# Every second piece of an up-projection's weights gets its low part from an adding DMA

## Chip, cores and metric

The kernel runs on one core of one Trainium2 chip. The metric is the device time of one execution in microseconds (us); the time before is the median of three runs, 1161.08 us (1160.6 to 1163.76). A core has a matrix engine (TensorE: PE in the profile, its weight loads PEld), VectorE (DVE), ScalarE (ACT), GpSimd (POOL), SyncE (SP), which here only issues DMAs, and 16 DMA engines. Each engine works through its own instructions in a fixed order; semaphores order the engines among each other.

## The reference, cut to what matters

One layer of a hybrid encoder, for 256 tokens of width 2048, everything in float32:

```
h  = rms_norm(x);  p = h @ w_in                      # 2048 x 6152
x  = x + concat(norm(fox_attention), norm(stick_breaking)) @ w_out
h  = rms_norm(x);  u = h @ w_up                      # 2048 x 11264
u  = causal_depthwise_conv(u, width 3) + conv_b
gate, val = split(u, 2)
x  = x + (silu(gate) * val) @ w_down                 # 5632 x 2048
```

The change sits in `u = h @ w_up`.

## The kernel before, in words

**Two parts.** TensorE is fed in a reduced 32-bit format (float32r). To keep the accuracy, each operand is split in two: a high part, the value rounded to that format, and a low part, the value minus the high part. A product is the sum of high times high, high times low and low times high.

**Pieces of weights.** All weights come through `weights` (L202): 204 pieces, mostly of 128 partitions x 2048 elements (1 MB). SP issues the load into `w_raw` (L209; three buffers), ScalarE rounds it into `w_hi` (L210; two buffers), VectorE writes `w_lo` = `w_raw` - `w_hi` (L211; two buffers), and TensorE multiplies. So a `w_raw` buffer is free for the load three pieces on once VectorE's L211 has read it, and a `w_hi` buffer is free once TensorE is through with the piece two before. The three instructions are given a priority that lets the scheduler place them ahead of other work (AHEAD = 200); the order on each engine is otherwise the scheduler's, fixed when the kernel is built.

**The up-projection.** `feature_major` (L244) computes two tiles of 128 features for the 256 tokens from two pieces (`kh` 0 and 1, each 8 row blocks of 128 x 256 columns, so rows of 1 KB in memory). A piece is 16 times a matmul with `w_hi` over both parts of the activations (512 columns, L258) and a matmul with `w_lo` over the high part (256 columns, L262), in this order: the first low matmul is the second matmul of a piece. The last argument `spare` is true in the up-projection alone, where there are 88 pieces. After two pieces, `convolved` (L580) takes the sums out of PSUM (ACT L586, DVE L587 and L588) and applies the convolution (ACT L590, DVE L594); after four, the gate is applied and split into `g2` (L615 to L619; 24 buffers).

**The order of the feed-forward.** Three parts of 16, 16 and 12 feature tiles (FFN_PARTS): up-projection of a part (32, 32 and 24 pieces), then its down-projection (`token_major`, L220; 16, 16 and 12 pieces). Before them stand the projections and attention, then the output projection, whose last column block is followed by squares of the rows (ACT L167) and by transposes that fill `hT` (PE L152, ACT L157, DVE L158) for the up-projection. The pool `ff` (L573) takes over the memory that the attention's pools had.

Of the kernel before, what the change touches and what calls it, by code (L numbers as in the profile page):

```python
# [9 lines left out]
F32R = mybir.dt.float32r  # L10
AF = mybir.ActivationFunctionType
ALU = mybir.AluOpType
# [16 lines left out]

# Columns of the constant array.  # L30
C_ID, C_TRI, C_ONE = (P * i for i in range(3))
# [12 lines left out]
def hybrid_layer(  # L44
# [34 lines left out]
    def f32(t):  # L79
        return t.bitcast(F32)  # L80

# [1 line left out]
    NC2 = 2 * NFT  # L83
# [48 lines left out]

# [1 line left out]
    pcol = const.tile([P, 50], F32, name="pcol")  # L134
# [12 lines left out]
    def transposed_split(k, g):  # L147
        """Feature tiles k and k + 1 of the tokens' rows, transposed, times g, in two parts."""
        ps = psb.tile([P, 2, S], F32, name="ps_x", tag="t")
        for j in range(2):  # L150
            for t in range(NT):
                nc.tensor.transpose(  # L152
                    ps[:, j, t * P : (t + 1) * P], xt[t][:, (k + j) * P : (k + j + 1) * P], ident
                )
        for j in range(2):
            i = k + j
            act.activation(hT[:, i, 0, :], ps[:, j, :], AF.Identity, scale=g[:, i : i + 1])  # L157
            dve.scalar_tensor_tensor(  # L158
                hT[:, i, 1, :], ps[:, j, :], g[:, i : i + 1], f32(hT[:, i, 0, :]),
                op0=ALU.mult, op1=ALU.subtract,  # L160
            )

    def sums_of_squares(ss, c):
        """Of 512 columns of each token tile."""
        for t in range(NT):
            junk = tmp.tile([P, 512], F32, name="junk", tag="raw", bufs=4)
            act.activation(junk, xt[t][:, c * 512 : (c + 1) * 512], AF.Square, accum_out=ss[:, t, c : c + 1])  # L167

    def token_factors(ss, n):
        """1 / rms of each token: per partition, and in every partition."""  # L170
        rstd = const.tile([P, NT], F32, name=f"rstd{n}")
        ssum = small.tile([P, NT], F32, name="ssum", tag="ssum")
        dve.tensor_reduce(ssum, ss, axis=AX.X, op=ALU.add)
        rsqrt(rstd, ssum, 1.0 / D, NT)
        dg = []
        for t in range(NT):
            dg.append(small.tile([P, P], F32, name="dg", tag="dg", bufs=2))
            dve.tensor_scalar(dg[t], ident, rstd[:, t : t + 1], None, op0=ALU.mult)
        return rstd, dg
# [8 lines left out]

# [1 line left out]
    waiting = deque()  # L190
# [9 lines left out]

# [1 line left out]
    def weights(src, a, b):  # L202
        raw = wpool.tile([P, 2048], F32, name="w_raw", tag="w_raw")
        hi = wpool.tile([P, 2048], F32R, name="w_hi", tag="w_hi", bufs=2)
        lo = wpool.tile([P, 2048], F32R, name="w_lo", tag="w_lo", bufs=2)
        n = a * b
        r3 = raw[:, :n].rearrange("p (a b) -> p a b", a=a)
        with tc.high_priority(offset=AHEAD):
            nc.sync.dma_start(r3, src)  # L209
            act.copy(hi[:, :n], raw[:, :n])  # L210
            dve.tensor_tensor(lo[:, :n], raw[:, :n], f32(hi[:, :n]), op=ALU.subtract)  # L211
        return (
            hi[:, :n].rearrange("p (a b) -> p a b", a=a),
            lo[:, :n].rearrange("p (a b) -> p a b", a=a),
        )
# [4 lines left out]
    def token_major(lhs, w, k0, nk, c0, cols, pieces=None, before=None):  # L220
        """[tokens, cols] = lhs.T @ w[k0:k0+nk, c0:c0+cols] for both token tiles."""
        acc = [psa.tile([P, 512], F32, name=f"acc{t}", tag="acc") for t in range(NT)]
        k = 0
        for n in pieces or [4] * (nk // 4):
            if before:
                before(k, n)
            hi, lo = weights(rows_of(w, k0 + k, n, c0, cols), n, cols)
            for i in range(n):
                first, last = k + i == 0, k + i == nk - 1
                lh = lhs(k + i)  # L230
                for t in range(NT):
                    lhi = lh[:, 0, t * P : (t + 1) * P]
                    llo = lh[:, 1, t * P : (t + 1) * P]
                    o = acc[t][:, :cols]
                    nc.tensor.matmul(o, lhi, hi[:, i, :], start=first, stop=False)  # L235
                    nc.tensor.matmul(o, lhi, lo[:, i, :], start=False, stop=False)  # L236
                    nc.tensor.matmul(o, llo, hi[:, i, :], start=False, stop=last)  # L237
            k += n
            step()
        return acc  # L240
# [3 lines left out]
    def feature_major(w, c0, spare):  # L244
        """Two tiles of features, each [features, tokens] in two summands."""
        nonlocal n_acc
        acc = []
        for j in range(2):
            pool, tag = (psa, "acc") if n_acc % 3 or not spare else (psb, "s")
            acc.append(pool.tile([P, 512], F32, name="pu", tag=tag))  # L250
        n_acc += 1
        for kh in range(2):
            hi, lo = weights(rows_of(w, 8 * kh, 8, c0, 2 * P), 8, 2 * P)
            for i in range(8):
                k = 8 * kh + i
                for j in range(2):
                    fs = slice(j * P, (j + 1) * P)
                    nc.tensor.matmul(  # L258
                        acc[j], hi[:, i, fs], hT[:, k].rearrange("p a b -> p (a b)"),
                        start=k == 0, stop=False,  # L260
                    )
                    nc.tensor.matmul(  # L262
                        acc[j][:, S:], lo[:, i, fs], hT[:, k, 0, :], start=False, stop=k == KT - 1
                    )
            step()
        return acc

    with ExitStack() as actx:
# [9 lines left out]
        def to_heads(dst, rows, t, scale):  # L278
            """Four heads' [tokens, dims] to [dims, tokens], times scale."""
            ps = psb.tile([P, 4, P], F32, name="ps_h", tag="t")  # L280
# [4 lines left out]
        def fox_rows(acc, dst, g):  # L285
            """Queries or keys of four heads: normalised, then transposed."""
            rows = []
# [19 lines left out]

        # The last four heads come when the projections are through with hT, and are used up
        # before its last rows are written again.
        oT = [at.tile([P, 2, S], F32R, name=f"oT{h}") for h in range(2 * NH - 4)]  # L310
# [3 lines left out]
        def attended(po, h, g, group):  # L314
            """Output of a head, [dims, tokens]: times its norm's weight in two parts, and its squares."""
            o = oT[group * NH + h]
# [10 lines left out]

# [1 line left out]
        # The first columns of weights are taken as x arrives.  # L329
        def opening(k, n):  # L330
# [52 lines left out]
        def gates():  # L383
            # log_sigmoid(y) = min(y, 0) - ln(1 + exp(-|y|))
            la = tmp.tile([P, NT, NH], F32, name="la", tag="la")
# [7 lines left out]
            yield  # L393
            # Cumulative log gates, the head h of row r*8+h, over the tokens.
            pc = psb.tile([P, 512], F32, name="pc", tag="t")
# [71 lines left out]

# [1 line left out]
        B0 = 3 * WF + NH  # L469
# [15 lines left out]
        def sb_head(h, qT, kT, v):  # L485
# [8 lines left out]
            mm(z1, identR, maskS, start=False, stop=True)  # L494
            # softplus(z) = max(z, 0) + ln(1 + exp(-|z|))
            e = tmp.tile([P, 3 * P], F32, name="e", tag="pr")
# [8 lines left out]
            yield  # L505
            # z - sum of softplus over the keys from s on: the exponent of the weights.
            for i in range(2):
# [22 lines left out]

# [1 line left out]
        ss2 = const.tile([P, NT, 4], F32, name="ss2")  # L532
# [38 lines left out]

# [1 line left out]
    ff = ctx.enter_context(tc.tile_pool(name="ff", bufs=2))  # L573
# [6 lines left out]
    def convolved(ps, f):  # L580
        """Feature tile f after the up-projection, its token factor and its convolution."""
        nonlocal n_up
# [16 lines left out]
    def up_pair(f0):  # L599
        """Two feature tiles."""  # L600
        nonlocal R
# [7 lines left out]
    for n_part, (f_lo, f_hi) in enumerate(FFN_PARTS):  # L609
        for f in range(f_lo, f_hi, 2):  # L610
            gate = up_pair(f)
            val = up_pair(NFT + f)
            for j in range(2):
                sg = ff.tile([P, S], F32, name="sg", tag="sg")
                act.activation(sg, gate[j], AF.Silu)  # L615
                dve.tensor_tensor(sg, sg, val[j], op=ALU.mult)
                g2 = ff.tile([P, 2, S], F32R, name="g2", tag="g2", bufs=24)
                act.copy(g2[:, 0, :], sg)
# [66 lines left out]
```

## Time and profile before

| | |
|---|---|
| median of three runs | 1161.08 us |
| span of the profiled execution, first to last instruction (the profile has no other time of it) | 1158.9 us |
| granted TensorE clock, mean | 1.000 |
| bytes moved by DMA | 211.40 MB, 182 GB/s over the span |
| DVE busy, ACT busy, POOL busy | 732.1, 559.1, 0.2 us |

How to read it: busy time is the union of an engine's instructions. A row of the timeline gives the start in us from the span's start, the duration in us, engine, line, operation, output <- inputs, shapes and, in brackets, the idle time of the engine before it with what ended it. Matmul rows overlap each other, since matmuls are pipelined: what a matmul costs is the distance of two starts, not its own duration. "us to landing" of a DMA runs from its issue to its completion.

### The profile page before, as it was taken

What the parts mean: (1) busy time and instruction counts of PE and PEld (TensorE: products, weight loads), DVE (VectorE), ACT (ScalarE), POOL (GpSimd) and SP (SyncE); (2) the same over time, 40 slices, a digit from 0 to 9 for tenths busy, and PEclk for the clock granted to TensorE, in tenths of its full rate; (3) what the DMA queues carried; (4) which work ended last, traced back from release to release, by engine and by line L of the source; (5) the groups of instructions that cost most, each with busy time, mean ns of one, the idle gap of its engine ahead of it and who ended that gap; (6) DMA issues with size and microseconds to landing.
All of it is one profiled execution on the core that took longest, in us unless ns stands there. A gap on an engine that the chain in (4) does not pass through costs nothing.

```text
span 1158.9 us, 14648 instructions
## 1 busy us (share of the span) xinstructions
PE 1147.0 (99%) x6002; PEld 980.7 (85%) x6002; DVE 732.1 (63%) x960; ACT 559.1 (48%) x716; POOL 0.2 (0%) x4
## 2 busy tenths in 40 slices
PE   7999999999999999999999999999999999999998
PEld 5998888888888888888888888888888888888886
DVE  4646656556465667777774547777775456777753
ACT  4644444445564555555553335555554334555531
POOL 0000000000000000000000000000000000000000
PEclk9999999999999999999999999999999999999999
DMA  6666545554444555555556555655556655555662
GB/s 226 212 219 204 179 149 181 158 171 150 159 158 151 182 170 194 182 182 183 183 189 199 191 182 183 196 194 190 182 185 198 197 183 182 183 188 184 192 231 76
DMA packets 162540, 211.40 MB, mean 182 GB/s; under 512 B 3736, under 2 KB 117546, under 8 KB 162474
## 3 DMA queue, kind: packets, MB, share of 16 engines
q1 hardware_dynamic: 162474, 210.47, 56.5%
q8 instruction: 47, 0.77, 0.3%
q14 instruction: 19, 0.16, 0.0%
HBM read 208.36 MB, written 2.10 MB: 182 GB/s over the span
## 4 chain that ended last, share of the span: by engine, by line
PE 97%; DVE 1%; ACT 1%; DMA 0%; issue 0%; SPq 0%
PE pu L258 33%; PE pu L262 17%; PE acc L235 14%; PE acc L237 14%; PE acc L236 14%; DVE w_lo L211 1%; ACT w_hi L210 1%; PE ps_x L152 1%; DMA x<-in_x_dram 0%; PE ps_h L282 0%; PE ps_z L491 0%; PE ps_s L423 0%; PE ps_o L517 0%; PE ps_o L450 0%; PE ps_p L444 0%
## 5 line engine op out<-in xcount | busy, mean ns | idle before, releaser
L211 DVE TENSOR_TENSOR w_lo<-w_raw,w_hi 128x2048 fp32r<-128x2048 f32 (+2 forms) x204 | 450.7, 2210 | 341.1 <-ACT w_hi L210 340.8
L258 PE MATMUL pu<-hT,w_hi 128*128 128x512 f32 x1664 | 586.0, 397 | 0.0
L210 ACT CAST w_hi<-w_raw 128x2048 fp32r<-128x2048 f32 (+2 forms) x204 | 375.7, 1842 | 368.1 <-PE acc L237 164.7
L262 PE MATMUL pu<-hT,w_lo 128*128 128x256 f32 x1664 | 466.6, 281 | 0.1
L258 PEld LDWEIGHTS pu<-hT,w_hi 128*128 128x128 f32 x1664 | 312.1, 188 | 73.7
L262 PEld LDWEIGHTS pu<-hT,w_lo 128*128 128x128 f32 x1664 | 314.3, 189 | 0.7 <-DVE w_lo L211 0.5
L237 PE MATMUL acc<-w_hi,g 128*128 128x512 f32 x352 | 139.0, 395 | 0.0
L235 PE MATMUL acc<-w_hi,g 128*128 128x512 f32 x352 | 138.9, 395 | 0.0
L236 PE MATMUL acc<-w_lo,g 128*128 128x512 f32 x352 | 138.9, 395 | 0.0
L235 PE MATMUL acc<-w_hi,hT 128*128 128x512 f32 (+1 forms) x320 | 119.8, 376 | 0.0
L236 PE MATMUL acc<-w_lo,hT 128*128 128x512 f32 (+1 forms) x320 | 119.1, 372 | 0.1
L237 PE MATMUL acc<-w_hi,hT 128*128 128x512 f32 (+1 forms) x320 | 118.9, 372 | 0.0
L594 DVE SCALAR_TENSOR_TENSOR cv<-up,ccol,cv 128x256 f32<-128x256 f32 x176 | 84.3, 479 | 1.6 <-ACT cv L590 0.7
L237 PEld LDWEIGHTS acc<-w_hi,g 128*128 128x128 f32 x352 | 66.3, 188 | 15.7 <-DVE g L619 0.2
L235 PEld LDWEIGHTS acc<-w_hi,g 128*128 128x128 f32 x352 | 66.3, 188 | 15.5
L236 PEld LDWEIGHTS acc<-w_lo,g 128*128 128x128 f32 x352 | 66.3, 188 | 15.4
L236 PEld LDWEIGHTS acc<-w_lo,hT 128*128 128x128 f32 x320 | 60.5, 189 | 9.0 <-DVE w_lo L211 0.9
L237 PEld LDWEIGHTS acc<-w_hi,hT 128*128 128x128 f32 x320 | 60.6, 189 | 8.7
L235 PEld LDWEIGHTS acc<-w_hi,hT 128*128 128x128 f32 x320 | 60.5, 190 | 8.2
L586 ACT COPY t<-pu 128x256 f32<-128x256 f32 x88 | 31.5, 360 | 58.8 <-PE pu L262 58.8
L590 ACT ACTIVATE cv<-up,ccol 128x256 f32<-128x256 f32 x88 | 52.6, 597 | 7.9 <-DVE up L588 5.6
L587 DVE TENSOR_TENSOR t<-pu,t 128x256 f32<-128x256 f32 x88 | 36.8, 420 | 21.9 <-ACT t L586 21.9
(148 smaller groups left out, 648.3 us busy)
## 6 DMA issues: line engine op xcount, KB each, us to landing
w_raw<-in_w_up_dram SPq DMA_DIRECT2D x88, 1024.0 KB, 5.1
w_raw<-in_w_down_dram SPq DMA_DIRECT2D x44, 1024.0 KB, 5.3
w_raw<-in_w_in_dram SPq DMA_DIRECT2D x36, 1024.0 KB, 5.2
w_raw<-in_w_out_dram SPq DMA_DIRECT2D x16, 1024.0 KB, 5.1
w_raw<-in_w_in_dram SPq DMA_DIRECT2D x12, 688.0 KB, 5.1
w_raw<-in_w_in_dram SPq DMA_DIRECT2D x8, 512.0 KB, 5.2
out_dram<-x SPq DMA_DIRECT2D x8, 256.0 KB, 5.3
x<-in_x_dram SPq DMA_DIRECT2D x3, 512.0 KB, 6.1
```

The source lines that it names most:

```text
L152: nc.tensor.transpose(ps[:, j, t * P : (t + 1) * P], xt[t][:, (k + j) * P : (k + j + 1) * P], ident)
L210: act.copy(hi[:, :n], raw[:, :n])
L211: dve.tensor_tensor(lo[:, :n], raw[:, :n], f32(hi[:, :n]), op=ALU.subtract)
L235: nc.tensor.matmul(o, lhi, hi[:, i, :], start=first, stop=False)
L236: nc.tensor.matmul(o, lhi, lo[:, i, :], start=False, stop=False)
L237: nc.tensor.matmul(o, llo, hi[:, i, :], start=False, stop=last)
L258: nc.tensor.matmul(acc[j], hi[:, i, fs], hT[:, k].rearrange("p a b -> p (a b)"), start=k == 0, stop=False,)
L262: nc.tensor.matmul(acc[j][:, S:], lo[:, i, fs], hT[:, k, 0, :], start=False, stop=k == KT - 1)
L586: act.copy(t2, ps[:, S:])
L587: dve.tensor_tensor(t2, ps[:, :S], t2, op=ALU.add)
L590: act.activation(a, u[:, 2:], AF.Identity, scale=ccol[:, 2, f : f + 1], bias=ccol[:, 3, f : f + 1])
L594: dve.scalar_tensor_tensor(a, u[:, w : w + S], ccol[:, w, f : f + 1], a, op0=ALU.mult, op1=ALU.add)
```

## The change

In the up-projection, every second piece (the first of each two, 44 in all) gets its low part in another way: ScalarE writes minus the high part into a new tile `w_ld` (three buffers in the pool `ff`), then a DMA that GpSimd issues reads the same weights from memory once more and adds them to what stands in `w_ld`. The high part is made as before. VectorE has no instruction for these pieces. `g2` has 22 buffers in place of 24. The diff, without its removed comments:

```diff
-    def weights(src, a, b):
+    n_pieces = 0
+
+    def weights(src, a, b, shared=False):
+        nonlocal n_pieces
+        n_pieces += shared
         raw = wpool.tile([P, 2048], F32, name="w_raw", tag="w_raw")
         hi = wpool.tile([P, 2048], F32R, name="w_hi", tag="w_hi", bufs=2)
-        lo = wpool.tile([P, 2048], F32R, name="w_lo", tag="w_lo", bufs=2)
+        by_dma = shared and n_pieces % 2
+        if by_dma:
+            lo = ff.tile([P, 2048], F32R, name="w_ld", tag="w_ld", bufs=3)
+        else:
+            lo = wpool.tile([P, 2048], F32R, name="w_lo", tag="w_lo", bufs=2)
         n = a * b
         r3 = raw[:, :n].rearrange("p (a b) -> p a b", a=a)
         with tc.high_priority(offset=AHEAD):
             nc.sync.dma_start(r3, src)
-            act.copy(hi[:, :n], raw[:, :n])
-            dve.tensor_tensor(lo[:, :n], raw[:, :n], f32(hi[:, :n]), op=ALU.subtract)
+            if by_dma:
+                act.activation(lo[:, :n], raw[:, :n], AF.Copy, scale=-1.0)
+                nc.gpsimd.dma_start(
+                    lo[:, :n].rearrange("p (a b) -> p a b", a=a), src, accum_op=ALU.add
+                )
+                act.copy(hi[:, :n], raw[:, :n])
+            else:
+                act.copy(hi[:, :n], raw[:, :n])
+                dve.tensor_tensor(lo[:, :n], raw[:, :n], f32(hi[:, :n]), op=ALU.subtract)
...
-            hi, lo = weights(rows_of(w, 8 * kh, 8, c0, 2 * P), 8, 2 * P)
+            hi, lo = weights(rows_of(w, 8 * kh, 8, c0, 2 * P), 8, 2 * P, spare)
...
-                g2 = ff.tile([P, 2, S], F32R, name="g2", tag="g2", bufs=24)
+                g2 = ff.tile([P, 2, S], F32R, name="g2", tag="g2", bufs=22)
```

## Prediction

> **What bounds the kernel now.** I read the page first (busy times, the chain that ended last, the costliest groups, the DMA queues), then a table by stage, then the timeline of one stretch of the up-projection.
>
> ```profile
> span 1158.9 us, 14648 instructions
> PE 1147.0 (99%) x6002; PEld 980.7 (85%) x6002; DVE 732.1 (63%) x960; ACT 559.1 (48%) x716; POOL 0.2 (0%) x4
> ...
> q1 hardware_dynamic: 162474, 210.47, 56.5%
> ...
> PE 97%; DVE 1%; ACT 1%; DMA 0%; issue 0%; SPq 0%
> ...
> L211 DVE TENSOR_TENSOR w_lo<-w_raw,w_hi 128x2048 fp32r<-128x2048 f32 (+2 forms) x204 | 450.7, 2210 | 341.1 <-ACT w_hi L210 340.8
> ...
> L262 PEld LDWEIGHTS pu<-hT,w_lo 128*128 128x128 f32 x1664 | 314.3, 189 | 0.7 <-DVE w_lo L211 0.5
> ```
>
> TensorE is 97% of the chain, and its low weights waited for VectorE (last row, the wait named at its end) for 0.5 us in the whole kernel. By stage:
>
> ```profile
> core 0: us, PE busy (x) PEld busy (x) DVE busy (x) ACT busy (x) POOL busy (x), PEclk, DMA share, GB/s
> 430.00:590.00 160.00, 160.00 (x907) 138.68 (x906) 120.13 (x173) 85.39 (x114) 0.00 (x0) 1.00 0.57 184
> 700.00:850.00 150.00, 150.00 (x867) 132.25 (x866) 112.92 (x161) 80.14 (x107) 0.00 (x0) 1.00 0.58 190
> ```
>
> These are two stretches of the up-projection. TensorE has no gap in either, VectorE is 75% busy (120.13 of 160) and the DMA engines 57%. So the VectorE time that the change takes away stands beside TensorE's and is worth nothing; what counts is whether weights still arrive in time. One stretch of ACT, DVE and SP, put together from their timelines, then the landing times, and the DMA rate in 40 slices of 0.6 us from 500 to 524:
>
> ```profile
> 499.88 1.91 ACT L210 CAST w_hi<-w_raw 128x2048 fp32r<-128x2048 f32 x1 [2.67 <-issue]
> 501.82 2.29 DVE L211 TENSOR_TENSOR w_lo<-w_raw,w_hi 128x2048 fp32r<-128x2048 f32 x1 [1.55 <-ACT w_hi L210]
> 504.14 0.37 SPq L209 DMA_DIRECT2D w_raw<-in_w_up_dram  x1
> 516.84 1.91 ACT L210 CAST w_hi<-w_raw 128x2048 fp32r<-128x2048 f32 x1
> ```
> ```profile
> DMA to landing us min/median/max: 5.1/5.2/5.2
> ```
> ```profile
> GB/s 266 386 387 384 253 32 0 0 29 159 375 384 384 352 65 0 0 0 72 230 386 386 387 289 12 0 0 32 193 384 391 387 324 36 0 0 10 111 355 384
> ```
>
> From 499.88 to 516.84 are three pieces: 5.65 us a piece, 11.3 us a pair. VectorE ends at 504.11, the load for the piece three on is issued at 504.14 and lands 5.2 us later at 509.3; its cast starts at 516.84. So the loads are **7.5 us ahead**. A load runs at some 386 GB/s while it moves, 2.7 us for 1.05 MB, and 2.5 us of the 5.2 are latency.
>
> **The change, part by part.**
>
> *VectorE* loses 44 subtractions of 2.29 us, 101 us: worth 0, since TensorE hides them. At most the 0.5 us of its wait above.
>
> *ScalarE* gains 44 copies of 1.91 us (as the cast), 84 us. In the stretch 430 to 590 it is busy 85.39 of 160 us, 6.0 us a pair; 7.9 of 11.3 then fits. But order counts. In the built kernel the minus copy of a DMA piece (call it 2m+1) stands on ScalarE *ahead* of the cast of the piece before it (2m). It waits for the load of 2m+1, so the cast of 2m, VectorE's subtraction and TensorE now wait for a load that they don't use. This closes a ring: the `w_raw` buffer for 2m+1 comes free with VectorE's subtraction of 2m-2; then follow issue 0.03, landing 5.2, minus copy 1.91, cast of 2m 1.91, subtraction of 2m 2.29, and the next turn begins. Sum: 0.03 + 5.2 + 1.91 + 1.91 + 2.29 = **11.34 us per pair, against 11.3** that TensorE needs. A dead heat, as long as no load gets slower: each us on that load is a us on every pair.
>
> *The added DMA* is not in this trace in any form: GpSimd issues none. It reads 1 MB from memory, reads 1 MB of minus parts and writes 1 MB. Bounds for its data time: that of one load, 2.7 us, if reading the old value costs nothing; 8.1 us if three movements follow one another. I take 5.4, two reads one after the other: the one of the load's kind is sure, and a write goes along with a read in every load here. Adding 44 x 5.4 us would fill the engines: 0.57 x 11.3 = 6.4 us a pair plus 5.4 is 11.8.
>
> The Trainium skill (Collectives: The Full Stack, "The bandwidth ceiling: the fold count and why AG ≠ RS ≠ AR") says that an adding transfer gets about half the rate of a copying one, because two sources are read, with a measured ratio of 1.93; no run here shows it yet. By it the data time would be an estimated 5.2 us, and the sum that follows would hardly move.
>
> *What it does to the loads.* In the ring the minus copy of 2m-1 ends 4.2 us (cast 1.91, subtraction 2.29) before the load of 2m+1 is issued. Issued as fast as SP's loads, the adding DMA's data would run from about 3.4 us before that issue; of 5.4 us some 1.2 would be left when the load's data starts 0.8 us after its issue, and the load would be 1.2 us late. Issued 1.5 us later or more (1,024 rows by an engine that has issued none), it lies beside the whole load, and at equal shares the load's 2.7 us become 5.4: **2.7 us late**. Lower end 0 (2.7 us of data, early issue, over before the load). I take 2.7, because the profile counts every queue against the same 16 engines, and those run at their full 386 GB/s under one load alone. Period: 11.3 + 2.7 = 14.0 us.
>
> Whether TensorE also waits for the adding DMA itself: from the end of the minus copy until TensorE comes to 2m+1 there are 1.91 + 2.29 + 5.65 = 9.85 us, and the pair has 2.7 us of slack besides. One stage further back, the minus copy of 2m+5 stands behind the cast of 2m+3, which waits until TensorE is through with 2m+1: two periods are at least landing time + 5.65 + 1.91 + 1.91. At 14.0 us the DMA may take 18.5 us from issue to landing; every us beyond costs half a us a pair. I expect about 11 and charge nothing.
>
> *The sum over pairs:* 44 x 2.7 = 119 us, less the lead of 7.5 us that each of the three parts can use up first (it comes back in the down-projections, which keep the old ring): 119 - 22.5 = **96 us**.
>
> *The start.* In the built kernel the first minus copy stands behind the last squares (L167) and one L157. The rows of before:
>
> ```profile
> 412.98 0.39 PE L258 MATMUL pu<-hT,w_hi 128*128 128x512 f32 x1
> 413.20 0.28 PE L262 MATMUL pu<-hT,w_lo 128*128 128x256 f32 x1
> 418.62 1.03 PE L152 MATMUL ps_x<-cs,x 128*128 128x128 f32 x8
> ```
> ```profile
> 416.18 0.19 ACT L167 ACTIVATION_READ_ACCUMULATOR junk<-x 128x1 f32 x1
> 420.52 0.82 ACT L157 ACTIVATE hT<-ps_x,pcol 128x256 fp32r<-128x256 f32 x2
> ```
>
> L167 ends at 416.4, one L157 (0.4) brings it to 416.8, the minus copy to 418.7, and with 5.2 + 2.7 us for the DMA the first low part is there at 426.6; before, TensorE used it at 413.2. Of the 13.4 us TensorE fills 1.7 with the transposes and small matmuls that the new order places ahead and with a gap it had anyway: **11.7 us**. Bounds: landing in 5.2 us gives 9.0; in 12 us, 16.
>
> *The rest* at 0: `g2` with 22 buffers needs the oldest back only at the 23rd tile, seven tiles into the second part, when the first down-projection, its reader, is over on TensorE. 44 of SP's waits for a free `w_raw` now end with ScalarE's cast instead of VectorE's subtraction, 2.3 us earlier; these loads queue behind that of the ring on SP anyway. The minus copy also waits for TensorE to be through with the `w_ld` of six pieces before, long over. Behind GpSimd's waits stands nothing but its next adding DMA.
>
> *Sum:* 1158.9 + 96 + 11.7 = 1266.6; the median stands 2.2 us above the span, so **1269 us**.
>
> **The rivals.**
>
> *Only the start* (the added DMA costs what a load does and is over before the next): x = 0, the ring ties, 9 us: 1170 us. For it: 43% of DMA time is free. Against: it needs both lower bounds. Chance 0.13. *Half hidden*: 1.2 us per pair, 44 x 1.2 = 53, less 22.5, plus 10: 1202 us, chance 0.15.
>
> *The adding DMA is the bound.* If its data takes 8.1 to 10.8 us, the engines need 6.4 + that, 14.5 to 17.2 us a pair; if it takes 23 us to land, the two-period ring gives (23 + 9.5) / 2 = 16.2. At 16.3: 44 x 5.0 - 22.5 + 16 = 213, so 1374 us. For it: 1 KB rows and a read-modify-write of unknown price. Against: nothing but the row of the load. Chance 0.24.
>
> *The clock.* TensorE's first matmuls here were slow:
>
> ```profile
> 11.13 0.63 PE L236 MATMUL acc<-w_lo,hT 128*128 128x512 f32 x1
> 11.56 0.63 PE L237 MATMUL acc<-w_hi,hT 128*128 128x512 f32 x1
> ...
> 17.17 0.39 PE L237 MATMUL acc<-w_hi,hT 128*128 128x512 f32 x1
> 17.40 0.39 PE L235 MATMUL acc<-w_hi,hT 128*128 128x512 f32 x1
> ```
>
> Starts are 0.43 us apart in the opening and 0.23 a few us later (the stage rows above have a granted clock of 1.00): over the 4.5 us or so of slow matmuls some 2.1 us lost. If every stall of 2.7 us brought that back, 44 x 2.1 = 92 us would come on top, 1361 us. But the slack of the ring (TensorE needs 11.3 of 14.0) covers 2.1 us, so this counts only if TensorE is again the bound. Chance 0.05. The Trainium skill (TensorE: Matmul & The Clock Gate, "Part 1: The HAM clock gate") has the clock halved after an idle window of about 3.4 us; the opening agrees with 0.43 against 0.23 us, and by that figure stalls of 2.7 us would mostly not trip it.
>
> *Not slower.* Matmuls of the output projection and pairs of the up-projection, then the subtraction beside them:
>
> ```profile
> 411.16 0.39 PE L236 MATMUL acc<-w_lo,hT 128*128 128x512 f32 x1
> ...
> 412.75 0.39 PE L237 MATMUL acc<-w_hi,hT 128*128 128x512 f32 x1
> ```
> ```profile
> 420.88 0.39 PE L258 MATMUL pu<-hT,w_hi 128*128 128x512 f32 x1
> ...
> 421.92 0.40 PE L258 MATMUL pu<-hT,w_hi 128*128 128x512 f32 x1
> ```
> ```profile
> 420.64 2.29 DVE L211 TENSOR_TENSOR w_lo<-w_raw,w_hi 128x2048 fp32r<-128x2048 f32 x1 [1.13 <-ACT w_hi L210]
> ```
>
> VectorE's stream might be what holds the up-projection's matmul pair at 0.353 us (5.65 / 16), where 768 columns at the first two rows' rate (seven starts in 1.59 us, 0.227 us for 512) would take 0.341. If taking it away freed all of this in the 704 pairs concerned and beside them (1408 in all), 17 us would come back, more than the start costs, with x = 0: 1153 us. It decides from 9 us on. Against it: beside a running subtraction (420.64 to 422.9) three pairs took 1.04 us, 0.347 each, so nearly all of the 0.353 stays. Chance 0.03. That the change doesn't do what it says I rule out: the built order has the 44 DMAs on GpSimd and 44 subtractions fewer.
>
> **How the numbers follow.** Forecast 0.40, half hidden 0.15, only the start 0.13, adding DMA as bound 0.24, clock 0.05, not slower 0.03. The forecast's own range is 1225 to 1320. Leaving out the lower part of "only the start", "not slower" and the upper part of the DMA bound (about 0.18 together) gives 1172 to 1390. A measurement of this kernel tells about 0.3% (3.5 us) from no change: faster 0.01, same 0.02, slower 0.97.
>
> **What would show it.** In the up-projection TensorE should have one gap of some 2.7 us per pair, ended by VectorE's subtraction of the *untouched* piece, with ScalarE's cast before it waiting behind the minus copy, and that copy for a load; loads of odd pieces landing in about 8 us, not 5.2; the start with a gap of 12 us ended by the adding DMA; VectorE 101 us lighter. Wrong would be: gaps ended mainly by the adding DMA (then it is the bound), no gaps (then the engines share better than assumed), or matmul starts 0.43 us apart.

## The result, and the profile after

The changed kernel takes **1324.04 us** (median of 4 runs, 1323.29 to 1325.98), the kernel before 1160.84 us beside it: a ratio of 1.139, 95% interval 1.137 to 1.142. The forecast was 1269 us in a range of 1172 to 1390: the right side, but 163 us were lost and not 108. The profiled execution has a span of 1322.7 us.

From the page of the changed kernel: busy times, the two DMA queues that matter (q1 holds SP's loads, q0 GpSimd's adding DMAs; packets, MB, share of 16 engines), the chain that ended last, the minus copy (L221), and the DMA issues with their median us to landing.

```profile
span 1322.7 us, 14759 instructions
PE 1201.1 (91%) x6002; PEld 1012.0 (77%) x6002; DVE 635.2 (48%) x916; ACT 640.3 (48%) x760; POOL 68.6 (5%) x48
...
q1 hardware_dynamic: 162474, 210.47, 48.9%
q0 software_dynamic: 45760, 46.14, 22.8%
...
PE 52%; DMA 25%; issue 8%; ACT 8%; DVE 6%; SPq 0%; ACTq 0%
...
L221 ACT ACTIVATE w_ld<-w_raw 128x2048 fp32r<-128x2048 f32 x44 | 84.2, 1915 | 232.7 <-DMA w_raw<-in_w_up_dram 232.7
...
w_raw<-in_w_up_dram SPq DMA_DIRECT2D x88, 1024.0 KB, 10.2
w_ld<-in_w_up_dram POOLq DMA_DIRECT2D x44, 1024.0 KB, 9.3
```

TensorE has fallen from 97% to 52% of the chain; a quarter of it is now the landing of loads. VectorE is 97 us lighter and ScalarE 81 us heavier, and neither is what costs. ScalarE's minus copy stood idle for 232.7 us, all of it for loads.

What TensorE waited for in the changed kernel (us in total, times, longest):

```profile
PE pu L279 <- DVE w_lo L228: 54.1, 35, 1.8
PE pu L275 <- ACT w_hi L227: 34.6, 21, 2.4
PE pu L279 <- issue: 8.6, 1, 8.6
PE pr L185 <- DVE dg L178: 8.0, 1, 8.0
...
PE pu L279 <- DMA w_ld<-in_w_up_dram: 4.2, 5, 1.0
```

L227 and L228 are the cast and the subtraction of the *untouched* piece. For the adding DMA itself TensorE waited 4.2 us. The rows of 8.6 and 8.0 us are the start, where the kernel before has no gap: from 413.8 us TensorE waits for factors of the norm, which stand behind two minus copies on ScalarE (L185 after L178), then until 431.56 for its first product with `w_ld` (the row that ends in "issue": the profile names nothing that ended it, but the first adding DMA, issued at 417.80, lands then, after 13.7 us). Together these waits are 110 of the 164 us by which the span grew; the other 54 are matmuls that ran slower (PE busy 1201.1 us against 1147.0), to which the paragraph on the clock comes back. The chain that ended last, between 533 and 560 us, is the forecast's ring (start, us, what):

```profile
533.84 9.27 DMA w_raw<-in_w_up_dram
...
543.20 0.09 ACT w_ld L221
543.29 1.73 issue
545.02 0.35 ACT t L603
545.37 1.81 ACT w_hi L227
...
547.21 2.29 DVE w_lo L228
...
549.52 7.87 DMA w_raw<-in_w_up_dram
...
557.48 0.06 ACT w_ld L221
```

Load, minus copy of the DMA piece (its rest is named issue here), cast of the untouched piece, subtraction, and with it the buffer for the next load. TensorE isn't in it. One turn is one pair of pieces, and its length is best read from GpSimd's issues, which come once a turn. The third and the last of the second part's 16, from GpSimd's timeline:

```profile
766.95 1.55 POOL L222 DMA_DIRECT2D w_ld<-in_w_up_dram  x1 [13.28 <-ACT w_ld L221]
...
961.65 1.57 POOL L222 DMA_DIRECT2D w_ld<-in_w_up_dram  x1 [14.24 <-ACT t L603]
```

(961.65 - 766.95) / 13 = **14.98 us a pair**, where the forecast had 14.0.

What makes the load slow is seen in the DMA view of two windows of that turn: 534 to 538 us, when the load issued at 533.84 should long be moving, and 539 to 543.

```profile
DMA packets 777, 0.80 MB, mean 199 GB/s; under 512 B 0, under 2 KB 777, under 8 KB 777
...
q0 software_dynamic: 767, 0.79, 122.6%
q1 hardware_dynamic: 10, 0.01, 0.9%
```
```profile
DMA packets 1445, 1.46 MB, mean 365 GB/s; under 512 B 19, under 2 KB 1445, under 8 KB 1445
...
q1 hardware_dynamic: 1441, 1.46, 108.5%
q0 software_dynamic: 4, 0.00, 0.2%
```

In this turn the two DMAs don't share. The adding DMA, which was issued first (at 530.05), has the 16 engines to itself, at 199 GB/s, until it is through; of 777 packets 10 are the load's. Then the loads run, at the usual rate. (A share above 100% means that an engine's packet times overlap.)

The up-projection's three parts, from TensorE's first matmul of a part to that of the next one (16, 16 and 12 pairs; the down-projections between them take 89.2 us in both kernels):

| part | before | after |
|---|---|---|
| first | 182.9 us | 245.8 us |
| second | 177.5 us | 237.9 us |
| third | 135.7 us | 177.2 us |

Before, TensorE thus needs 177.5 / 16 = 11.09 us a pair in the second part and 135.7 / 12 = 11.31 in the third; in the first it is 11.31 too, once the first two pairs are over. What sets the two paces is open.

### The profile page after: what moved, and what is told of

Same layout as the page of the kernel before. It is cut to its first block, busy times and chain, and to the rows that moved or that the text cites. A ratio compares the mean times of both kernels' runs of the same rounds, so it can differ in the third digit from the quotient of the medians.

```text
span 1322.7 us, 14759 instructions
## 1 busy us (share of the span) xinstructions
PE 1201.1 (91%) x6002; PEld 1012.0 (77%) x6002; DVE 635.2 (48%) x916; ACT 640.3 (48%) x760; POOL 68.6 (5%) x48
## 3 DMA queue, kind: packets, MB, share of 16 engines
q0 software_dynamic: 45760, 46.14, 22.8%
## 4 chain that ended last, share of the span: by engine, by line
PE 52%; DMA 25%; issue 8%; ACT 8%; DVE 6%; SPq 0%; ACTq 0%
DMA w_raw<-in_w_up_dram 25%; PE acc L252 11%; PE acc L254 11%; PE acc L253 11%; PE pu L275 10%; ACT w_hi L227 7%; PE pu L279 5%; DVE w_lo L228 5%; ACT w_ld L221 1%; PE ps_x L152 0%; ACT t L603 0%; DMA x<-in_x_dram 0%; PE ps_h L299 0%; PE ps_z L508 0%; PE ps_s L440 0%
## 5 line engine op out<-in xcount | busy, mean ns | idle before, releaser
L275 PE MATMUL pu<-hT,w_hi 128*128 128x512 f32 x1664 | 624.5, 414 | 34.6 <-ACT w_hi L227 34.6
L228 DVE TENSOR_TENSOR w_lo<-w_raw,w_hi 128x2048 fp32r<-128x2048 f32 (+2 forms) x160 | 349.9, 2187 | 418.6 <-ACT w_hi L227 418.4
L227 ACT CAST w_hi<-w_raw 128x2048 fp32r<-128x2048 f32 (+2 forms) x160 | 290.9, 1818 | 232.4 <-PE acc L254 151.8
L279 PE MATMUL pu<-hT,w_lo 128*128 128x256 f32 x960 | 291.1, 303 | 54.3 <-DVE w_lo L228 54.1
L279 PEld LDWEIGHTS pu<-hT,w_lo 128*128 128x128 f32 x960 | 200.1, 208 | 66.1 <-DVE w_lo L228 66.1
L279 PE MATMUL pu<-hT,w_ld 128*128 128x256 f32 x704 | 199.2, 283 | 12.8 <-issue 8.6
L221 ACT ACTIVATE w_ld<-w_raw 128x2048 fp32r<-128x2048 f32 x44 | 84.2, 1915 | 232.7 <-DMA w_raw<-in_w_up_dram 232.7
L279 PEld LDWEIGHTS pu<-hT,w_ld 128*128 128x128 f32 x704 | 133.7, 190 | 16.1 <-issue 8.8
L222 POOL DMA_DIRECT2D w_ld<-in_w_up_dram x44 | 68.4, 1556 | 1160.7 <-ACT w_ld L221 859.9
L225 ACT CAST w_hi<-w_raw 128x2048 fp32r<-128x2048 f32 x44 | 83.6, 1899 | 28.0 <-PE pu L275 18.6
```

The source lines that it names most:

```text
L221: act.activation(lo[:, :n], raw[:, :n], AF.Copy, scale=-1.0)
L222: nc.gpsimd.dma_start(lo[:, :n].rearrange("p (a b) -> p a b", a=a), src, accum_op=ALU.add)
L275: nc.tensor.matmul(acc[j], hi[:, i, fs], hT[:, k].rearrange("p a b -> p (a b)"), start=k == 0, stop=False,)
L279: nc.tensor.matmul(acc[j][:, S:], lo[:, i, fs], hT[:, k, 0, :], start=False, stop=k == KT - 1)
```

## The experiments

**Theory:** the minus copy, ahead of another piece's cast on ScalarE, closes a ring through the load; the adding DMA's data delays that load, and each us of delay is a us a pair. **Rivals:** the order alone costs the time, whatever the DMA does; the adding DMA itself is what TensorE waits for; or TensorE pays, through its clock. The kernel before took 1160.4 to 1160.9 us beside the runs that follow.

### E1: no adding DMA

```
                 act.activation(lo[:, :n], raw[:, :n], AF.Copy, scale=-1.0)
-                nc.gpsimd.dma_start(
-                    lo[:, :n].rearrange("p (a b) -> p a b", a=a), src, accum_op=ALU.add
-                )
```

> The minus copies stay where they are on ScalarE, the adding DMAs are left out (so the low parts of these pieces are only minus the high parts). My theory: the ring through the load, the minus copy, the cast of the untouched piece and the subtraction takes 15.0 us a pair only because the adding DMA slows the ring's load (landing 8 to 9.3 us in place of 5.2). Without it the ring is back at 11.3 to 11.6 us: 1163 to 1175 us. Rival, the order on ScalarE or its 44 extra copies are dear by themselves: over 1200 us.

Measured: 1181.06 us, ratio 1.018 (1.013 to 1.023); the four runs spread from 1175 to 1189, so it is clear that something is lost, but not whether it is more than 2%. The chain still turns in the same ring; from its rows between 510 and 550 us, the loads in it:

```profile
514.70 5.17 DMA w_raw<-in_w_up_dram
...
525.95 5.53 DMA w_raw<-in_w_up_dram
...
537.84 5.19 DMA w_raw<-in_w_up_dram
...
549.12 5.21 DMA w_raw<-in_w_up_dram
```

The ring without any delay turns in (549.12 - 514.70) / 3 = 11.47 us; the forecast's sum for it was 11.34. That is above what TensorE needs in any part, and the order alone costs about 20 us, some 6 more than the top of what was expected. The other 143 us need the DMA.

### E2 and E3: half of the adding DMA, and a plain copy in its place

```
-    lo[:, :n].rearrange("p (a b) -> p a b", a=a), src, accum_op=ALU.add
+    lo[:, : n // 2].rearrange("p (a b) -> p a b", a=a // 2), src[:, : a // 2, :], accum_op=ALU.add,   (E2)
+    lo[:, :n].rearrange("p (a b) -> p a b", a=a), src                                                 (E3)
```

> The adding DMA covers the first four of eight row blocks (the other half of the low part stays minus the high part). 512 packets in place of 1024: 3.4 us of the engines' time instead of 6.7. My theory: about 2.6 us of it have passed when the ring's load starts to move, 0.8 are left, so the load is 0.8 us late: period about 12.3, in all 1180 to 1205 us. Rival, a fixed price per DMA that GpSimd issues: over 1280 us.

> The same 44 DMAs from GpSimd, 1 MB each, but copying and not adding (the low part of these pieces becomes the weight itself). A packet should then take about 51 ns like a load's instead of 105: 3.3 us of the engines' time in place of 6.7. My theory: the same as with half the adding DMA, 1180 to 1205 us. Rival, the second load from memory or GpSimd's issuing is what costs: 1290 us or more.

Measured: E2 1197.17 us, ratio 1.031 (1.030 to 1.033); E3 1196.09 us, ratio 1.031 (1.028 to 1.033). The queue and the landing in each page, E2 and then E3:

```profile
q0 software_dynamic: 23232, 23.07, 13.0%
...
w_ld<-in_w_up_dram POOLq DMA_DIRECT2D x44, 512.0 KB, 5.9
```
```profile
q0 software_dynamic: 45760, 46.14, 17.6%
...
w_ld<-in_w_up_dram POOLq DMA_DIRECT2D x44, 1024.0 KB, 5.7
```

Adding half the bytes and copying all of them land within 0.2 us of each other and cost the same: an adding DMA has no price per DMA that stands out, it takes the engines for twice as long per byte. The copy moves 391 GB/s while it has them alone (525 to 526 us of E3), the adding DMA 199. (The shares in the queue rows don't show this factor; packet times overlap.) And the 127 to 128 us between either and the changed kernel are the second half of the engines' time. What E2 and E3 cost above E1 is mostly the start: their first parts take 205.4 and 201.0 us, E1's 188.0. In E3's chain between 510 and 550 us the ring's loads land as if there were no other DMA:

```profile
514.93 5.25 DMA w_raw<-in_w_up_dram
...
526.61 5.09 DMA w_raw<-in_w_up_dram
...
537.84 5.47 DMA w_raw<-in_w_up_dram
```

That fits DMA engines that, in this order of arrival, finish what came first. In E3 GpSimd issues the copy at 522.48 and its packets end at 527.5; the load issued at 526.61 has its first packets at 527.6, which is when they are due (in the kernel before they follow the issue by 1.0 to 1.2 us). Data of 2.8 us is through before the load needs the engines, data of 5.3 us is not.

### E4 and E5: TensorE with less and with more work

```
+    if spare and kh == 0:                                       (E4: those low products left out)
+        continue
```
```
+    for again in range(2 if spare and kh == 0 else 1):          (E5: those low products taken twice)
```

> All DMAs and copies stay, but TensorE leaves out the 704 low matmuls of the DMA pieces, so nothing waits for an adding DMA and TensorE has 1.9 us less per pair. My theory (the ring bounds, TensorE's half clock is covered by its slack): the period stays at 15.0 us and only the wait at the start goes, 1300 to 1318 us. Rival 1, TensorE at half clock is part of the bound: 44 x 1.9 to 2 x 1.9 us less, 1160 to 1240 us. Rival 2, the adding DMA's landing is part of the bound: likewise under 1250 us.

> E4 had also changed the order on ScalarE: in 35 of 44 cases the minus copy stood behind the cast of the untouched piece, not ahead of it, so it told nothing of TensorE. Here the order stays that of the changed kernel, and TensorE gets more work: the low matmuls of the DMA pieces are done twice (so these low parts count double), 1.9 us more per pair, 13.2 of the 15.0 us. My theory (the ring bounds, TensorE has slack): 1315 to 1340 us. Rival, TensorE or its half clock is part of the bound: 44 x 1.9 us more, about 1400 us.

Measured: E4 1192.54 us, ratio 1.029 (1.026 to 1.032), far off what either theory expected. ScalarE's timeline of E4 shows why:

```profile
508.92 1.90 ACT L227 CAST w_hi<-w_raw 128x2048 fp32r<-128x2048 f32 x1
...
510.72 1.91 ACT L221 ACTIVATE w_ld<-w_raw 128x2048 fp32r<-128x2048 f32 x1
...
512.83 1.90 ACT L225 CAST w_hi<-w_raw 128x2048 fp32r<-128x2048 f32 x1
```

With other matmuls the scheduler set ScalarE's order anew: in 35 of 44 pairs the minus copy stands *behind* the cast of the untouched piece (L227). The ring was open, by accident, and with it went the time. As a test of TensorE the run says nothing.

E5 kept the order: 1315.61 us, ratio 1.134 (1.133 to 1.136). TensorE has 704 matmuls more and the kernel isn't slower, so TensorE isn't the bound. E5's mean granted clock is 0.991 against 0.959; the better clock didn't matter either, beyond at most the 8 us by which E5 is faster. Where these come from is open.

### E6: the minus copy behind the cast before it

```
+    tc.add_manual_dep(neg.ins, last_cast.ins.name, ...)      # an order for the scheduler, no wait
```

> The changed kernel with one edge for the scheduler: each minus copy stands behind the cast of the piece before it, in 43 of 44 cases. The ring is open. What is left: the DMA engines (E4 carried all of it in 12.1 us a pair), and now the landing of the adding DMA: the minus copy starts when the cast of the untouched piece ends, at the earliest 1.9 us after TensorE is through with the piece two before, so a pair takes at least 1.9 + 1.9 + 9.3 (landing) = 13.1 us. My theory: 13.1 us a pair, 1215 to 1255 us, with TensorE now waiting for the adding DMA. Rival, the DMA engines bound the changed kernel: no change, over 1300 us.

Measured: **1371.51 us**, ratio 1.182 (1.179 to 1.185): slower than the change, and a plain miss. TensorE's waits, and the DMA's landing in the page of E6:

```profile
PE pu L285 <- DMA w_ld<-in_w_up_dram: 149.6, 21, 7.9
```
```profile
w_ld<-in_w_up_dram POOLq DMA_DIRECT2D x44, 1024.0 KB, 13.8
```

The ring through the cast is gone, and another wait has taken its place. GpSimd's timeline of E6, and the DMA view from 523 to 525 us:

```profile
520.99 1.57 POOL L228 DMA_DIRECT2D w_ld<-in_w_up_dram  x1 [9.64 <-ACT w_ld L222]
```
```profile
q1 hardware_dynamic: 754, 0.76, 107.4%
q0 software_dynamic: 7, 0.01, 1.6%
```

SP issues a load at 521.18, 0.2 us after GpSimd begins; in the changed kernel GpSimd is 3.8 us ahead (530.05 against 533.84). GpSimd takes 1.57 us to issue, so now the loads come first and the adding DMA waits, until 526; it lands in 13.8 us instead of 9.3, from a later start. The early minus copy had a use: it hid the adding DMA. E4 fits this: with E6's order in 35 of 44 pairs, and no product that needs an adding DMA, it took 1192.54 us.

But the queues don't always take turns. From 518 to 522 us of the same run, the adding DMA issued at 509.80, whose packets began at 514.7 behind an earlier load, and the load issued at 513.58 move side by side:

```profile
q0 software_dynamic: 469, 0.48, 74.2%
q1 hardware_dynamic: 461, 0.47, 43.2%
```

Sharing of this kind is what the prediction had assumed for the ring's load; in the changed kernel's turns it isn't there.

### E7: DMA pieces loaded into buffers of their own

```
+    if by_dma:
+        raw = ff.tile([P, 2048], F32, name="w_rd", tag="w_rd", bufs=2)
+    else:
         raw = wpool.tile([P, 2048], F32, name="w_raw", tag="w_raw")
-    lo = ff.tile([P, 2048], F32R, name="w_ld", tag="w_ld", bufs=3)
+    lo = ff.tile([P, 2048], F32R, name="w_ld", tag="w_ld", bufs=2)
-    g2 = ff.tile([P, 2, S], F32R, name="g2", tag="g2", bufs=22)
+    g2 = ff.tile([P, 2, S], F32R, name="g2", tag="g2", bufs=18)
```

> The weights of the DMA pieces are loaded into two buffers of their own (paid for with 18 buffers of g2 in place of 22 and two of w_ld in place of three), so their load waits for ScalarE's cast of four pieces before and no longer for VectorE's subtraction; the minus copy stays ahead of the cast. The ring is open and the adding DMA starts early. Left is what the DMA engines need, 12.1 us a pair in E4: 1195 to 1220 us. Rival, the DMA engines' time adds up by packets (2 x 3.3 + 6.7 = 13.3 us a pair): 1240 to 1260 us. Rival, the order alone counts: over 1300 us.

Measured: 1178.7 us, ratio 1.016 (1.015 to 1.018), better than expected. All 44 adding DMAs are there. The chain's shares and the landing from the page of E7, then its row in the table by stretch (PE, PEld, DVE, ACT, POOL busy; clock, DMA share, GB/s):

```profile
PE 95%; DMA 2%; DVE 1%; ACT 1%; issue 0%; SPq 0%; ACTq 0%
...
w_ld<-in_w_up_dram POOLq DMA_DIRECT2D x44, 1024.0 KB, 10.0
```
```profile
460.00:590.00 130.00, 130.00 (x749) 114.03 (x748) 73.42 (x130) 90.33 (x106) 17.08 (x11) 1.00 1.16 280
```

TensorE has no gap, at 11.15 us a pair (178.4 us for the 16 pairs of the second part). The DMA moves as many bytes and lands no sooner than in the changed kernel; only the load no longer waits for the subtraction of the piece before. So the ring is the cause, and the delayed load its length. The engines are near their end: data of two loads (2 x 2.7 us) and one adding DMA (5.3) makes 10.7 of 11.15 us.

### E8 and E9: the first two DMA pieces left as they were

```
-    by_dma = shared and n_pieces % 2
+    by_dma = shared and n_pieces % 2 and n_pieces > 4        (E8: alone; E9: with E7)
```

> The first two pairs of the up-projection keep the old way, 42 adding DMAs in place of 44. My theory: the wait at the start (12 us) goes, and two pairs less pay 3.7 us: 1300 to 1310 us. Rival, the start costs little and the first wait only moves to the third pair: 1314 to 1320 us.

> E7 with the first two pairs done the old way. In E7 a pair took 11.15 us, as TensorE needs it, and what was left above the kernel before (18 us) is the start, where TensorE waited 9.7 us for the first adding DMA and before that for the load into a buffer that only then came free. My theory: with the start gone the kernel is back at the time of before: 1157 to 1167 us, no version of it clearly faster, since VectorE was never the bound. Rival 1, VectorE's relief is worth something once the waits are gone: under 1155 us. Rival 2, the wait moves to the first DMA piece wherever it stands: over 1172 us.

Measured: E8 1305.24 us, ratio 1.125 (1.123 to 1.127); E9 1161.97 us, ratio 1.000 (0.999 to 1.001). E8's first part takes 227.1 us, 18.7 less than in the changed kernel; two pairs without the ring's extra 3.67 us (14.98 - 11.31) are 7.3 of it, and the start is the other 11.4. From E9's page:

```profile
span 1159.3 us, 14733 instructions
...
PE 1144.9 (99%) x6002; PEld 978.6 (84%) x6002; DVE 639.1 (55%) x918; ACT 634.7 (55%) x758; POOL 65.6 (6%) x46
```

E9 does what the change is about, with 42 adding DMAs and VectorE 93 us lighter than before, and takes as long as the kernel before; the 18 us that E7 lost were its start. So VectorE's relief is worth nothing, as far as can be measured.

### E10: the kernel before with 22 buffers for `g2`

```
-    g2 = ff.tile([P, 2, S], F32R, name="g2", tag="g2", bufs=24)
+    g2 = ff.tile([P, 2, S], F32R, name="g2", tag="g2", bufs=22)
```

> The kernel before with 22 buffers of g2 in place of 24, nothing else. My theory: worth nothing, 1158 to 1164 us. Rival: part of the loss is in it, over 1166 us.

Measured: 1160.16 us, ratio 0.999 (0.998 to 1.000). The smaller pool costs nothing.

## Why the prediction was right, and where its size was off

**The ring: right.** Its links stand in the chain above in the order given, TensorE's gaps are ended by the subtraction and the cast of the untouched piece, and E7, which opens the ring and keeps all the adding DMAs, takes 145 of 163 us away. (It pays with fewer buffers for `g2` and `w_ld`; E9, with the same buffers, shows that this costs nothing.)

**The adding DMA's data time: right.** 5.4 us was taken; 1.05 MB at 199 GB/s are 5.3 (6.1 from its first packet to its last in the turn shown, as it starts slowly). Plain loads reach 385 GB/s in the same turn, a ratio of 1.94. The Trainium skill (Collectives: The Full Stack, "The bandwidth ceiling: the fold count and why AG ≠ RS ≠ AR") puts ReduceScatter, which adds, at about half the rate of AllGather, which copies, 1.93 by its measurement, because the add needs two source reads: the ratio in the traces agrees.

**The load's delay: the step that failed.** The prediction had the load beside the adding DMA, "at equal shares the load's 2.7 us become 5.4: 2.7 us late". In the turns read here there are no shares: the load waits until the adding DMA's last packets, and the load of the other piece, issued 0.5 us behind it in these two turns, then runs beside it. The two loads quoted landed in 9.27 and 7.87 us, 8.6 on average, so 3.4 us late. The prediction did weigh the better picture, an adding DMA that goes first and delays the load by its rest, but with an issue as fast as SP's it came to 1.2 us. In the trace the first packets come 2.3 us after GpSimd begins to issue (530.05, 532.3; the issue alone takes 1.55 us, SP's 0.37) and the last at 538.4; the load's first, due at 534.9, come at 537.7. So 2.7 us lay near the truth by luck: what the prediction added up, a transfer at half rate, isn't what delays the load.

Two smaller terms join it. The ring without delay is 11.47 us (E1) and not 11.34: every second turn has a copy of the convolution (L603, 0.35 us in the chain) between minus copy and cast. And the prediction's 11.3 us a pair, read in the first part, holds there and in the third, but in the second TensorE needs only 11.09. So a pair costs 14.98 - 11.31 = 3.67 us more in these two parts and 14.98 - 11.09 = 3.89 in the second, not 2.7: 0.7 from the landing, 0.1 from the copy, in the second part 0.2 from TensorE's pace, and some 0.2 that the two quoted turns don't show.

**The lead that is used up first: twice too high.** 28 x 3.67 + 16 x 3.89 is 165 us. The three parts lost 62.9 + 60.4 + 41.5 = 165 us, 11.4 of them by the start, so 153 by the ring: a credit of some 12 us, not 22.5. The second part shows 1.8 of it and the third 2.5, where 7.5 each was taken; the reason is open.

**The start: the size right, the picture only in part.** 11.4 us from E8, against 11.7. But the first low part was there at 431.5 us and not at 426.6: the first adding DMA landed in 13.7 us, where 7.9 was taken and 12 was the upper bound, as two loads moved ahead of it (SP issues them at 416.43 and 417.50, its own first packets come at 423.0). TensorE stood idle for 16.6 us, in two waits. That the price lies so close to the forecast is luck.

**The adding DMA is covered: right, by less than it seemed.** It landed in 9.3 us, where 11 was expected and 18.5 was held to be bearable. TensorE waited 4.2 us for it in all, the start aside. E6 shows that the cover hangs on the early minus copy.

**The rivals.** "Adding DMA is the bound", at 1374 us, lies as near to the result as the forecast does, and is wrong: its data takes 5.3 us and not 8 to 11, and E7 carries it at TensorE's own pace. "Only the start" and "half hidden" needed a shorter data time. E2 and E3, with half of it, come out at 1197 and 1196 us, so the two bounds of the prediction were the right ones to ask about. "Not slower" falls with E9: a lighter VectorE gives TensorE nothing. Its 0.353 us for a pair of matmuls is the pace of 11.31 us; the second part before runs at 11.09 with all of VectorE's subtractions, and E9 at 178.4 / 16 = 11.15 without half of them.

**The clock: covered, as forecast, but it did fall.** The up-projection from the table by stretch of the changed kernel (columns as for E7):

```profile
460.00:630.00 170.00, 143.70 (x754) 121.03 (x753) 71.71 (x130) 88.80 (x102) 17.07 (x11) 0.95 0.90 214
```

0.95, where before and in E7 it is 1.00. The waits quoted above are at most 2.4 us long, the start aside. The Trainium skill (TensorE: Matmul & The Clock Gate, "Part 1: The HAM clock gate") has the clock halved after an idle window of about 3.4 us, from which the prediction took that stalls of 2.7 us would mostly not trip it; here shorter ones did. The trace's record of the clock shows how: it is at half 19 times after the start, for 3.41 or 6.83 us each, and in the 3.41 us before each fall TensorE stood idle for 1.8 to 2.9 us in all, in one or two gaps; no other such 3.41 us at the full clock, counted in the same steps, held more than 1.84. The slower matmuls are the 54 us of the section on the result. The ring's slack took them up: TensorE is busy 143.70 of 170 us with them, and E5, with more matmuls and a clock of 0.991, is only 8 us faster.

**No cost for the loads that now come earlier: too simple.** The prediction set the 44 loads whose buffer ScalarE frees at 0, as they queue behind the ring's load on SP. They do, but close behind it, and then run beside it. How much of the 3.4 us is theirs was not taken apart.

## What to carry to other kernels

An instruction that waits for its own data, put ahead of others' work on an engine that runs in order, can tie that work to a buffer ring which it had nothing to do with; add the ring up link by link, and compare it with what the bound engine needs per turn. A DMA that is issued earlier can delay a later one by all that is left of it, as in the changed kernel, so what a new DMA costs depends on whether it is through before the next load's data would start. Relief for an engine that isn't on the chain was worth nothing here, 93 us of it.

## What the runs showed of the hardware

- **DMAs of two queues ran one after the other in the changed kernel, and side by side elsewhere.** In the changed kernel, 767 of 777 packets in the four us after the load's issue were the adding DMA's. In E6 469 and 461 packets of the two queues moved in the same four us, and at E7's start 1507 and 1563 between 427 and 440 us. The Trainium skill (DMA: Bandwidth & Descriptors, "Queues, rings and completion order") says that a DMA engine switches between queues after a whole packet, of some 9 to 17 descriptors as a rule and 64 at most. An adding DMA has 45760 / 44 = 1040 records, 65 for each of 16 engines; so a packet at that upper end would fit the changed kernel's turns, and a smaller one E6 and E7. What decides between the two, no run here shows.
- **An adding DMA moves 199 GB/s where a load moves up to 385.** There is no further price that shows: half of one costs what a whole copy does.
- **GpSimd takes longer to issue a DMA that adds:** 1.56 us against 0.88 for the same 1,024 rows copied (E3), from the two kernels' groups of costliest instructions:

```profile
L222 POOL DMA_DIRECT2D w_ld<-in_w_up_dram x44 | 68.4, 1556 | 1160.7 <-ACT w_ld L221 859.9
```
```profile
L222 POOL DMA_DIRECT2D w_ld<-in_w_up_dram x44 | 38.6, 877 | 1063.1 <-ACT w_ld L221 839.9
```

- **TensorE's clock fell with gaps of at most 2.4 us**, to 0.95 in the up-projection, where the idle time within 3.41 us came to 1.8 us or more. TensorE wasn't the bound, and E5 leaves 8 us at most as its price.
